# Squared distance of rows: a second load ahead of the entry barrier, and the result stored by two queues

## The chip, the cores and the metric

The kernel runs on one core of a Trainium2 chip. The metric is the device time of one execution in microseconds, of which the median of several runs is given. A profile is taken of one execution; its span goes from the first instruction to the last one on the core, and the device time also holds what lies around that span.

## The reference

```python
batch, dim = 1024, 4096
x, y = float32 [1024, 4096], float32 [1024, 4096]

def reference(x, y, axis):          # axis = -1
    return np.sum((x - y) ** 2, axis=axis).astype(np.float32)
```

Two arrays of 16.78 MB each are read, and 1024 numbers, 4 KB, are written.

## The kernel before

**Layout.** Partition p holds the 8 rows 8p to 8p+7 of x and y side by side, 32,768 columns in all (lines 60 and 61). The result is a tile `results` of 128 partitions by 8 columns, one column for each row of a partition, and goes back to the output with 32 bytes per partition (line 62).

**Loads.** SP issues all of them, in one queue, through the helper `load` (line 106 to 109), each with a semaphore of its own that counts to 16. The columns of x are cut in eight loads (`xw`, line 72), those of y in ten (`yw` and two narrow ones that are kept for the end, lines 73 and 74). The loop at lines 111 to 117 makes the order: x0 (4096 columns), x1 (12288), y0 (16256), x2, y1, and so on to two last y loads of 192 and 128 columns. X and Y hold six rows each (H, line 65), so loads beyond the sixth row wait on SP until the squares of the first two rows are done (line 220).

**The entry barrier.** Every engine begins with a drain and a barrier that all engines pass together. `Program.early` (line 29) takes the instructions that were recorded so far and puts them into the entry block, ahead of the named engine's first drain. Line 120 records one load, x0, and line 121 moves it ahead of SP's drain. SP issues the remaining loads after the barrier (lines 122 and 123).

**Arithmetic.** DVE waits for the loads of a piece and subtracts in place (`sub`, line 175); ACT waits for that difference, squares it and adds it up along the columns (`square`, line 181), one number for each piece; where a row has several pieces DVE adds these numbers (`complete`, line 188). The very last piece is squared and summed on DVE itself (line 204). All writers of `results` that end last count on the semaphore `sums`.

**The end.** SP waits until `sums` has its full count, issues the store of the whole tile (lines 231 and 232), clears the program's semaphores in one range (`close`, line 44) and waits for the store's 16 increments on `stored` (line 45). The semaphores that are cleared are those made by `prog.semaphore`, a range from the first to the last; `stored` is not among them and is counted back to 0 by the last wait.

Of the kernel before, what the change touches and what calls it, by code (L numbers as in the profile page):

```python
# [47 lines left out]
def kernel(tc, x, y, axis, out):  # L48
    nc = tc.nc
    P = nc.NUM_PARTITIONS  # L50
# [11 lines left out]
    ov = out.rearrange("(p r) -> p r", p=P)  # L62
# [5 lines left out]
    results = nc.alloc_sbuf_tensor("results", [P, R], F32).ap()  # L68
# [22 lines left out]
    prog = Program(nc, tc)  # L91
    stored = nc.alloc_semaphore("stored")
    diffs = prog.semaphore("diffs")
    acts = prog.semaphore("acts")
    sums = prog.semaphore("sums")
    n = dict(diffs=0, acts=0, sums=0)

    def home(c0, c1):
        h0 = c0 % H
        return slice(h0, h0 + c1 - c0)  # L100
# [5 lines left out]
    def load(landed, src, dst, name, c0, c1):  # L106
        sem = prog.semaphore("%s%d" % (name, len(landed)))
        nc.sync.dma_start(out=dst[:, home(c0, c1)], in_=src[:, c0:c1]).then_inc(sem, 16)  # L108
        landed.append(((c0, c1), sem))
# [7 lines left out]
        order.append((landed_y, yv, Y, "y", c0, c1))  # L117

    todo = list(order)
    load(*todo.pop(0))  # L120
    prog.early(mybir.EngineType.SP)
    while todo and todo[0][5] <= H:
        load(*todo.pop(0))
# [62 lines left out]
    def complete(r):  # L186
        nc.vector.wait_ge(acts, squared[row_parts[r][-1]])
        nc.vector.tensor_reduce(  # L188
            out=results[:, r : r + 1],
            in_=parts_of(r, len(row_parts[r])),  # L190
            axis=mybir.AxisListType.X,
            op=add,
        ).then_inc(sums, 1)
        n["sums"] += 1

    for j, (c0, c1) in enumerate(ys):
        final = j == len(ys) - 1
        wait_loaded(c1, landed_y[j][1])
        for piece in pieces_of(j, c0, c1):
            sub(*piece)  # L200
            r = piece[0] // D
            if final:
                nc.vector.wait_ge(diffs, n["diffs"])
                nc.vector.tensor_tensor_reduce(  # L204
                    out=Y[:, home(*piece)],
# [22 lines left out]
                complete(r)  # L228
    complete(7)

    nc.sync.wait_ge(sums, n["sums"])
    nc.sync.dma_start(out=ov, in_=results).then_inc(stored, 16)
    prog.close(nc.sync, stored, 16)


# [33 lines left out]
```

## Time and profile before

| | us |
|---|---|
| median of three runs | 84.13 (83.96 to 84.15) |
| the profiled execution, device time | 83.96 |
| the profiled execution, span | 82.63 |
| DVE busy | 36.8 |
| ACT busy | 33.4 |
| first DMA packet starts | 0.998 |
| the last load has landed | 80.25 |
| the last reduction ends | 81.15 |
| SP issues the store | 81.18 |
| the store's 16 increments land | 82.43 to 82.60 |

A row of the span's 40 slices gives the busy share of each slice in tenths; a slice is 2.07 us long. DMA packets count in the slice in which they start. SP's DMA-issuing instructions do not count as busy time; their rows stand in the timeline as SPq. In the text, x0, x1, y0 and so on are the loads in the order in which the kernel makes them for each array.

### The profile page before, as it was taken

The numbers are of one execution on the slowest core, as the hardware profiler recorded it, in microseconds if no ns is written. First come the engines' busy times: TensorE is split into PE (matmuls) and PEld (weight loads), VectorE is DVE, ScalarE is ACT, GpSimd is POOL, SyncE is SP. The second block draws the span as 40 slices with busy tenths as digits, with TensorE's granted clock in tenths as the row PEclk, the third lists the DMA queues.
The fourth block names the chain that finished last, engine by engine and source line by source line (L and its number), as shares of the span: only waits on it lengthen the run. The fifth ranks groups of instructions, "written<-read, shape, count | busy, mean of one in ns | idle before, by whom it ended". The sixth has DMA issues, their size and how long they took to land.

```text
span 82.6 us, 136 instructions
## 1 busy us (share of the span) xinstructions
DVE 36.8 (45%) x27; ACT 33.4 (40%) x41; POOL 0.2 (0%) x4
## 2 busy tenths in 40 slices
DVE  0000000000000000000299999999189996989992
ACT  3300000000000000000000979889896999899991
POOL 0000000000000000000000000000000000000000
DMA  5998998888999991999599699969979799999960
GB/s 127 389 500 381 595 547 381 381 381 381 504 504 504 504 504 63 441 504 504 254 508 508 286 476 508 476 286 508 423 339 509 339 437 440 426 402 416 395 220 2
DMA packets 2736, 33.56 MB, mean 406 GB/s; under 512 B 432, under 2 KB 1328, under 8 KB 1712
## 3 DMA queue, kind: packets, MB, share of 16 engines
q1 hardware_dynamic: 2736, 33.56, 95.9%
HBM read 33.55 MB, written 0.00 MB: 406 GB/s over the span
## 4 chain that ended last, share of the span: by engine, by line
DMA 63%; SPq 16%; DVE 12%; ACT 4%; issue 1%
DMA Y<-in_y_dram 63%; SPq L108 16%; DVE X L175 11%; ACT X L181 4%; DVE Y L204 0%; DVE results L188 0%; SPq L220 0%; DVE results L204 0%
## 5 line engine op out<-in xcount | busy, mean ns | idle before, releaser
L175 DVE TENSOR_TENSOR X<-X,Y 128x2048 f32<-128x2048 f32 (+10 forms) x21 | 36.2, 1780 | 44.3 <-DMA Y<-in_y_dram 44.3
L181 ACT ACTIVATE X<-X 128x2048 f32<-128x2048 f32 (+9 forms) x20 | 31.2, 1559 | 46.1 <-DVE X L175 46.0
L181 ACT ACTIVATION_READ_ACCUMULATOR X<-X 128x1 f32 x20 | 3.7, 186 | 0.0
L181 ACT ACT_TABLE_LOAD x1 | 1.3, 1283 | 1.4 <-PEq L19 1.4
L188 DVE TENSOR_REDUCE results<-parts 128x1 f32<-128x2 f32 (+2 forms) x4 | 0.4, 152 | 0.0
L204 DVE CUSTOM_DVE_ANT_0 Y<-X,parts 128x128 f32<-128x128 f32 x1 | 0.4, 352 | 0.0
L250 POOL MEMSET const-bfloat16-1.0<- 128x1 bf16 x1 | 0.1, 101 | 0.0
L250 POOL MEMSET const-uint8-127<- 128x1 uint8 x1 | 0.1, 101 | 0.0
L250 POOL MEMSET const-float32-0.0<- 128x1 f32 x1 | 0.1, 98 | 0.2 <-issue 0.2
L250 POOL MEMSET const-float32-1.0<- 128x1 f32 x1 | 0.1, 98 | 0.0
L204 DVE DVE_READ_ACCUMULATOR2_ANT results<- 128x1 f32 x1 | 0.1, 83 | 0.0
## 6 DMA issues: line engine op xcount, KB each, us to landing
Y<-in_y_dram SPq DMA_DIRECT2D x1, 8128.0 KB, 39.0
X<-in_x_dram SPq DMA_DIRECT2D x1, 6144.0 KB, 20.2
X<-in_x_dram SPq DMA_DIRECT2D x1, 4096.0 KB, 48.3
Y<-in_y_dram SPq DMA_DIRECT2D x1, 4096.0 KB, 57.5
X<-in_x_dram SPq DMA_DIRECT2D x1, 2736.0 KB, 13.3
X<-in_x_dram SPq DMA_DIRECT2D x1, 2048.0 KB, 7.1
Y<-in_y_dram SPq DMA_DIRECT2D x1, 1392.0 KB, 19.0
Y<-in_y_dram SPq DMA_DIRECT2D x1, 1312.0 KB, 16.1
```

The source lines that it names most:

```text
L108: nc.sync.dma_start(out=dst[:, home(c0, c1)], in_=src[:, c0:c1]).then_inc(sem, 16)
L175: nc.vector.tensor_sub(out=a, in0=a, in1=Y[:, home(c0, c1)]).then_inc(diffs, 1)
L181: nc.scalar.activation(out=a, in_=a, func=Square, accum_out=acc).then_inc(acts, 1)
L188: nc.vector.tensor_reduce(out=results[:, r : r + 1], in_=parts_of(r, len(row_parts[r])), axis=mybir.AxisListType.X, op=add,).then_inc(sums, 1)
L204: nc.vector.tensor_tensor_reduce(out=Y[:, home(*piece)], in0=X[:, home(*piece)], in1=X[:, home(*piece)], scale=1.0, scalar=parts_of(r, 1), ...
L250: nc = _bacc.Bacc("TRN2", target_bir_lowering=False, num_devices=1)
```

## The change

Two edits. The loop that records loads ahead of `early` now takes two loads, x0 and x1, so that SP issues both ahead of its drain for the entry barrier and starts with y0 behind it. At the end, the store is cut by partitions: ACT waits for the sums, issues the store of partitions 64 to 127 on its own queue and then counts a new semaphore `begun`; SP waits for the sums, issues the store of partitions 0 to 63, waits for `begun`, and then clears the semaphores and waits for 32 increments of `stored`. `begun` keeps SP from clearing `sums` before ACT has passed its wait for it.

```diff
@@ -93,6 +93,7 @@
     sums = prog.semaphore("sums")
+    begun = prog.semaphore("begun")
     n = dict(diffs=0, acts=0, sums=0)
@@ -117,7 +118,8 @@
     todo = list(order)
-    load(*todo.pop(0))
+    for _ in range(2):
+        load(*todo.pop(0))
     prog.early(mybir.EngineType.SP)
     while todo and todo[0][5] <= H:
         load(*todo.pop(0))
@@ -228,9 +230,15 @@
     complete(7)
 
+    half = P // 2
+    nc.scalar.wait_ge(sums, n["sums"])
+    nc.scalar.dma_start(out=ov[half:P], in_=results[half:P]).then_inc(stored, 16)
+    nc.scalar.sem_inc(begun, 1)
     nc.sync.wait_ge(sums, n["sums"])
-    nc.sync.dma_start(out=ov, in_=results).then_inc(stored, 16)
-    prog.close(nc.sync, stored, 16)
+    nc.sync.dma_start(out=ov[0:half], in_=results[0:half]).then_inc(stored, 16)
+    nc.sync.wait_ge(begun, 1)
+    prog.close(nc.sync, stored, 32)
```

## The prediction

> **What bounds the kernel now.** I read the 40 slices first, then the chain of waits, then the two ends of the span closely, because the change touches only those ends.
>
> ```profile
> DMA  5998998888999991999599699969979799999960
> GB/s 127 389 500 381 595 547 381 381 381 381 504 504 504 504 504 63 441 504 504 254 508 508 286 476 508 476 286 508 423 339 509 339 437 440 426 402 416 395 220 2
> DMA 63%; SPq 16%; DVE 12%; ACT 4%; issue 1%
> ```
>
> The DMA engines carry the program: 33.55 MB, with hardly an empty slice. The zeros and low digits inside the row are packets counted at their start (a packet of the second load lasts 1.8 us), not pauses. Only the first slice and the last two are really thin. So I cut the span by hand into windows (columns: length, busy time of DVE, ACT and POOL, granted clock, DMA share, GB/s):
>
> ```profile
> 0.00:0.99 0.99, 0.00 (x0) 0.00 (x0) 0.20 (x4) 1.00 0.00 0
> 7.00:21.00 14.00, 0.00 (x0) 0.00 (x0) 0.00 (x0) 1.00 0.91 393
> 21.00:79.75 58.75, 35.48 (x22) 30.94 (x35) 0.00 (x0) 1.00 1.01 428
> 80.05:82.01 1.96, 1.04 (x5) 0.91 (x6) 0.00 (x0) 1.00 0.00 0
> 82.01:82.23 0.22, 0.00 (x0) 0.00 (x0) 0.00 (x0) 1.00 0.35 19
> 82.23:82.63 0.40, 0.00 (x0) 0.00 (x0) 0.00 (x0) 1.00 0.00 0
> ```
>
> The reader is to see three parts. First 0.99 us in which nothing moves (the first packet starts at 0.998). Then 79 us in which the loads flow. Then a tail from 80.05 on: 1.1 us of arithmetic on the last pieces and 1.4 us of storing. The tail in the chain of waits (start, length, what) and the store's row among the DMA issues (from the start of its issue to its landing, 1.4 us):
>
> ```profile
> 66.94 13.12 DMA Y<-in_y_dram
> 80.05 0.02 issue
> 80.08 0.57 DVE X L175 x2
> 80.65 0.03 issue
> 80.67 0.35 DVE Y L204
> 81.03 0.01 DVE results L204
> 81.03 0.12 DVE results L188
> out_dram<-results SPq DMA_DIRECT2D x1, 4.0 KB, 1.4
> ```
>
> **The head: the second load ahead of the barrier.** SP's rows in the timeline of the first microseconds:
>
> ```profile
> 0.00 0.38 SPq L108 DMA_DIRECT2D X<-in_x_dram  x1
> 1.43 0.33 SPq L108 DMA_DIRECT2D X<-in_x_dram  x1
> 1.81 0.44 SPq L108 DMA_DIRECT2D Y<-in_y_dram  x1
> ```
>
> SP issues x0, its drain for the barrier starts at 0.425 and is the last to arrive, and the barrier (three rounds, line 19 and line 250) lets it go on to x1 at 1.433: 1.008 us from drain to next issue. After the change x1 is issued at 0.425, so the drain starts one issue and one gap later, 0.328 + 0.048 = 0.376, at 0.801. 1.008 later, at 1.81, comes y0, where it stands now (1.812). By the dearer issue row (0.436 for y0) it would be 1.92. So x1 is issued 1.008 us earlier, y0, x2 and y1 0 to 0.11 later, and the other engines leave the barrier 0.38 to 0.49 later.
>
> What is x1 worth 1.008 us earlier? Nothing, I say: x0 occupies all 16 engines until x1's packets follow at 6.5 without a gap (its landings are complete at 7.12), and x1 at 1.433 is 5 us ahead of its turn already. The cover is those 5 us of x0; with x0 over before 2.43 (1.433 plus the 0.998 that x0 needs to its first packet), the gain would be up to 1.008. The barrier's 0.38 to 0.49 falls on POOL's constants, on DVE, first needed at 40.86, and on ACT's table load, 1.438 plus 1.283, which moves to about 1.8 to 3.1 while ACT's first square is at 45.32: 42 us of cover. y0 is issued at 1.8 to 1.9 for a turn after 21. Against a gain stands one possible loss: x1's issue now runs before x0's first packet exists (0.998), where it ran at 1.433 beside the flow. The rows nearest are y0's, x2's and y1's issues from 1.8 to 3.2: the packets that start beside them take 0.61 to 0.65 us, as later ones do (0.61). So I take 0, and keep +0.38 (x0's first packet pushed back by a whole issue and gap) for the range. I find no gain here below 0.
>
> **The tail: two stores.** The path of the store now, from the trace's single rows: the last reduction ends at 81.149; SP's issue starts at 81.177 (0.348 long); the first packet starts at 82.019 (0.842 after the issue's start); 144 packets, 9 on each of 16 engines, have started by 82.213 (0.194); the last increment of the store's semaphore lands at 82.60 (0.387 after the last packet); SP's last wait is through at 82.613.
>
> SP's half. The issue and the way to the first packet are taken as they are. An issue here does not grow with the bytes: 0.328 for x1 (49,152 bytes a partition), 0.377 for x0 (16,384), 0.348 for the store (32). But each makes one packet for each of 128 partitions, so this trace can't exclude that it grows with partitions; then up to half the issue, 0.174, is saved. Each engine has 4 rows and not 8. One engine's 8 rows take about 0.047 (first packet of all 82.019, first completion packet 82.066), half of that is 0.024. SP's half thus lands 0.02 earlier, at best 0.20.
>
> ACT's half. ACT is idle from 80.957 and waits for the same count at 81.149, so it starts at 81.18 as SP does. No row shows a DMA issued by ACT. The bounds are SP's two ways to a first packet on idle DMA engines: 0.842 (the store, 18 issues into the program) and 0.998 (x0, the first issue of its queue, a load). ACT's store is the first on its queue, so I take 0.998: +0.156. Then 82.175 + 0.194 - 0.024 = 82.345 for its last packet and 0.387 more to land: 82.732, against 82.60. That is **+0.13**; with 0.842 it is -0.02.
>
> The completions: one semaphore takes 32 increments and not 16. The 16 now arrive between 82.43 and 82.60, about one every 11 ns. Bounds: 0, if increments of two stores interleave as the last two loads' did (between 80.01 and 80.05 their landings overlap at no slower rate), or a second 0.17 behind the first. With ACT 0.156 later the two rows of increments lie end to end anyway, so I take 0 and keep +0.17.
>
> Do the two halves get in each other's way on the engines? The window 82.01 to 82.23 above shows the store's packets filling 0.35 of 0.22 us on 16 engines, so two thirds of that time is free and the halves can lie beside each other: 0.
>
> A rule stands against this edit. The Trainium skill, "DMA: Bandwidth & Descriptors", section "Rules for kernel authors", says not to bother with two transfers to disjoint partition halves, since both spray over the same engines and serialize; taken strictly, ACT's 0.17 of packets would follow all of SP's and the sum would be an estimated 0.17 worse than by the window's row.
>
> The waits added. SP's wait for ACT's issue (begun): behind it on SP stand only the clearing of semaphores (now 81.577, 0.068 long) and the final wait, and nobody waits for those. ACT's increment should come at 81.18 + 0.377 + 0.05 = 81.61, so the clearing ends near 81.7, hidden under the landing at 82.6 to 82.7; the cover is 0.9 us. ACT's wait for the sums has only the store and that increment behind it.
>
> Sum on the profiled execution: 0 (head) + 0.13 (ACT's half) + 0 (increments, begun) = span 82.63 + 0.13 = 82.76; with the 1.33 us that lie around the span (83.96 - 82.63) 84.09. That execution was the fastest of three, 0.17 under the median, so against the median it is 84.13 + 0.13, about **84.27**.
>
> **The rivals.** About 0.3% (0.25 us) is what a measurement of this kernel can tell from no change.
>
> First, ACT's half is as quick as SP's warm store and halving pays: from -0.02 (packets alone) to -0.20 (issue by partitions too), so 83.93 to 84.11. For it: both engines are idle and released at the same time, the 16 DMA engines are empty. Against: the issue rows show no growth with bytes, and ACT's queue is unused before. Even at its best it stays inside 0.25 us; only with a head effect that I can't see would it be faster.
>
> Second, slower: the second store's completions come behind the first's. Its place is the stretch from 82.2 to 82.6, its price 0.17 for 16 increments more on top of ACT's 0.156 later start, 0.33 less 0.02, so 84.44. It decides as soon as ACT's first packet and the queueing together exceed 0.25, hence ACT's 0.156 with 0.12 of queueing is enough. For it: the final wait needs all 32, the later of two queues counts, and nothing else lies beside it. Against: the overlap at 80.01 to 80.05.
>
> Third, x1's early issue holds back x0's first packet by up to 0.38: every load moves by it, since the flow has no slack, and the time is 84.13 + 0.38 = 84.51, with ACT's 0.13 as much as 84.64. Against: the issue rows beside running packets.
>
> Fourth, the early issue really feeds the engines sooner: bounded by 1.008 (83.12), with 5 us of x0 in front of it very unlikely.
>
> **How the numbers follow.** Forecast (a loss of about 0.13, not tellable from none; own range 84.15 to 84.38) 0.45; ACT quick 0.22; second store's completions behind 0.18; x0 held back 0.11; the gain at the head 0.04. Faster by over 0.3%: the last case and half of ACT's quick case at its best end with scatter of the medians, 0.14. Slower: both slower cases, 0.29, and 0.09 of the forecast's upper edge, 0.38. The rest, 0.48, is within 0.3%. The range goes from 83.92 (ACT quick at its best) to 84.62 (x0 held back and ACT late).
>
> **What would show it.** Right: x0's first packet near 1.0 and x1's issue at 0.43, y0's issue at 1.8 to 1.9, no gap between x0's and x1's packets, the last load landing at 80.25 as now; in the tail an ACT issue starting at 81.18 with its first packet 0.9 to 1.0 later and the last of 32 increments at 82.7. An ACT packet as early as SP's speaks for the first rival; increments of one store waiting for the other's for the second; x0's first packet at 1.3 for the third. Wrong altogether would be the prediction if ACT's first issue costs something that no row of SP's shows (the one thing ACT fetches in this trace, its table, takes 1.28), or if the 1.33 us outside the span change because a second queue is in use.

## The result and the profile after

The changed kernel takes 84.70 us in the median (84.57 to 84.73), the kernel before 84.04 in the runs beside it: a ratio of 1.0076, 95% interval 1.0056 to 1.0096, or some 0.65 us slower. The forecast of 84.27 and the upper end of its range, 84.62, were both too low.

The profiled execution took 84.73 us with a span of 83.39, against 83.96 and 82.63: 0.76 us longer; what lies outside the span is as before (1.34 and 1.33). The first windows of the changed kernel's span (columns: stretch, length, DVE, ACT, POOL busy, granted clock, DMA share, GB/s) look as they did before:

```profile
0.00:1.00 1.00, 0.00 (x0) 0.00 (x0) 0.20 (x4) 1.00 0.00 0
7.00:21.00 14.00, 0.00 (x0) 0.00 (x0) 0.00 (x0) 1.00 0.92 398
21.00:79.75 58.75, 35.28 (x21) 30.69 (x35) 0.00 (x0) 1.00 1.00 426
```

Nothing moves in the first microsecond (first packet 1.008, before 0.998), and the flow has the same rate. SP's rows in the timeline show that x1's issue moved (it is the second of the two):

```profile
0.00 0.86 SPq L109 DMA_DIRECT2D X<-in_x_dram  x2
1.92 0.33 SPq L109 DMA_DIRECT2D Y<-in_y_dram  x1
```

The end of the chain of waits of the changed kernel (start, length, what):

```profile
67.19 13.10 DMA Y<-in_y_dram
80.29 0.02 issue
80.31 0.57 DVE X L177 x2
80.89 0.03 issue
80.91 0.35 DVE Y L206
81.26 0.01 DVE results L206
81.27 0.09 DVE results L190
```

The arithmetic behind the last loads is the same, but starts 0.23 us later. It waits for the last load but one, which landed at 80.292 and not at 80.052; the last one landed at 80.505 and not at 80.251. The last reduction ends at 81.362 instead of 81.149, which is 0.21 of the 0.76 us. The other 0.55 lie behind it. The two store issues in the timeline, their rows among the DMA issues (last column: us from the start of the issue to the landing), and the windows around their packets:

```profile
81.39 0.53 SPq L239 DMA_DIRECT2D out_dram<-results  x1
81.39 0.54 ACTq L236 DMA_DIRECT2D out_dram<-results  x1
```

```profile
out_dram<-results SPq DMA_DIRECT2D x1, 2.0 KB, 1.7
out_dram<-results ACTq DMA_DIRECT2D x1, 2.0 KB, 2.0
```

```profile
81.39:82.55 1.16, 0.00 (x0) 0.00 (x0) 0.00 (x0) 1.00 0.00 0
82.55:82.74 0.19, 0.00 (x0) 0.00 (x0) 0.00 (x0) 1.00 0.20 11
82.74:82.82 0.08, 0.00 (x0) 0.00 (x0) 0.00 (x0) 1.00 0.00 0
82.82:83.01 0.19, 0.00 (x0) 0.00 (x0) 0.00 (x0) 1.00 0.20 11
83.01:83.39 0.38, 0.00 (x0) 0.00 (x0) 0.00 (x0) 1.00 0.00 0
```

The reader is to see two things that no row of before had. Both engines are released together, at 81.39, but an issue of half as many partitions takes 0.53 and 0.54 us and not 0.35, and SP's first packet starts 1.17 us after the issue's start and not 0.84. And the packets come in two groups with an empty stretch between them: ACT's first packet starts 1.434 us after its issue's start, 0.27 behind SP's.

So three questions were open. Was the later last load the work of the early x1? Why is SP's own half slower? Why is ACT's half later still?

### The profile page after: what moved, and what is told of

It is laid out like the page before. It is cut to its first block, busy times and chain, and to the rows that moved or that the text cites. A ratio compares the mean times of both kernels' runs of the same rounds, so it can differ in the third digit from the quotient of the medians.

```text
span 83.4 us, 138 instructions
## 1 busy us (share of the span) xinstructions
DVE 36.7 (44%) x27; ACT 33.4 (40%) x41; POOL 0.2 (0%) x4
## 4 chain that ended last, share of the span: by engine, by line
DMA 63%; SPq 16%; DVE 12%; ACT 4%; issue 1%
DMA Y<-in_y_dram 63%; SPq L109 16%; DVE X L177 11%; ACT X L183 4%; DVE Y L206 0%; DVE results L190 0%; SPq L222 0%; DVE results L206 0%
```

## The experiments

Edits are against the kernel before unless another is named, `...` marks lines left out (the line that makes the semaphore `begun` is left out throughout), and ratios are against the kernel before in runs on the same chip. "Tail" is the time from the first store issue's start to the last increment of the store's semaphore: 1.42 us before (81.177 to 82.597), 1.97 in the changed kernel (81.390 to 83.358).

**The early load alone.**

```diff
-    load(*todo.pop(0))
+    for _ in range(2):
+        load(*todo.pop(0))
```

> The second load ahead of the barrier, the store as before. Theory 'held back': x1's issue at 0.425 us, straight behind x0's, pushes back x0's packets on the one DMA engine served last (in the changed kernel its first packet started at 1.864 us, the latest one before at 1.491), that engine stays behind to the end, and the last load lands 0.2 to 0.3 us later than before (80.45 to 80.55, not 80.25), time +0.2 to +0.3 us. Rival 'accident': the late engine was this one execution's, the last load lands at 80.25 within 0.1, time within 0.1 us of before. Rival 'gain': x1 earlier feeds the engines sooner, last load before 80.2, time below before.

The ratio is 1.0000 (0.9986 to 1.0014), medians 84.15 and 84.16. The profiled execution happened to be the slowest of the kernel's twelve (84.47), and its last load landed later than that of any other profile:

```profile
67.53 13.06 DMA Y<-in_y_dram
80.59 0.02 issue
80.61 0.57 DVE X L176 x2
```

The last load lands at 80.755 here, later than either theory said, and between 80.25 and 80.58 in the profiles of all kernels with one early load (80.47 with the split alone). The sixteenth packet of the program, the last before the engines begin their second ones at 2.1, starts at 1.862 here and 1.864 in the changed kernel, but at 1.887 in the kernel with one early load and the split store: it is not x1 that delays it. The scatter is there from the first load on: x0 has landed at 7.12 to 7.15 us in five of the profiles with one early load and at 7.28 to 7.41 in the other six; with two early loads it was 7.33 and 7.35. So "held back" falls, since its 0.2 to 0.3 us lie outside the interval of the ratio (0.12 us either way), and "accident" holds in its time: the landing of the last load scatters by some tenths from one execution to the next, the kernel before had been profiled at the early end of that (80.25), and the early load costs and brings nothing that these runs can tell.

**The split alone.** The change's second edit without its first (the edit is against the changed kernel):

```diff
-    for _ in range(2):
-        load(*todo.pop(0))
+    load(*todo.pop(0))
```

> Only x0 ahead of the barrier, the store split. If the two edits add, this has the rest of the 0.76 us by which the changed kernel's span is longer: last load at 80.25, end of the last reduction to end of span 2.0 us (before 1.48), time +0.5 to +0.6 us. If the split alone is cheap and only its meeting with the early load was dear, +0.13 us as predicted.

Ratio 1.0064 (1.0045 to 1.0083), median 84.72; by the ratio 0.54 us over before: all of the loss, within the interval. The tail is 1.96 us, with the same issues (0.525 and 0.542) and first packets (1.171 and 1.436) as in the changed kernel. The last load was 0.2 later than in the profile of before here too, which again belongs to the scatter.

**The whole store from ACT.**

```diff
-    nc.sync.wait_ge(sums, n["sums"])
-    nc.sync.dma_start(out=ov, in_=results).then_inc(stored, 16)
+    nc.scalar.wait_ge(sums, n["sums"])
+    nc.scalar.dma_start(out=ov, in_=results).then_inc(stored, 16)
+    nc.scalar.sem_inc(begun, 1)
+    nc.sync.wait_ge(begun, 1)
     prog.close(nc.sync, stored, 16)
```

> The whole store, 128 partitions, from ACT's queue alone; SP issues nothing there. Theory 'new queue': ACT's first DMA is slow by itself, issue about 0.54 us and first packet 1.2 to 1.4 us after the issue's start, time +0.4 to +0.6 us. Theory 'shared': only two issues at the same time slow each other, so this has an issue of 0.35 to 0.38 us, a first packet after 0.84 to 1.0 us, time 0 to +0.16 us.

Ratio 1.0003 (0.9989 to 1.0017). The windows of the store:

```profile
81.25:82.12 0.87, 0.00 (x0) 0.00 (x0) 0.00 (x0) 1.00 0.00 0
82.12:82.33 0.21, 0.00 (x0) 0.00 (x0) 0.00 (x0) 1.00 0.37 20
82.33:82.73 0.40, 0.00 (x0) 0.00 (x0) 0.00 (x0) 1.00 0.00 0
```

ACT's first DMA of the whole program takes 0.370 us to issue and 0.871 to its first packet, against 0.348 and 0.842 on SP; the tail is 1.44. ACT's queue, used for the first time, costs 0.02 to 0.03 us over SP's here, and "new queue" falls.

**One half from SP alone.** The lower half is stored as in the change, nothing by ACT; the upper half of the result is left out.

```diff
-    nc.sync.dma_start(out=ov, in_=results).then_inc(stored, 16)
+    nc.sync.dma_start(out=ov[0:64], in_=results[0:64]).then_inc(stored, 16)
```

> SP stores partitions 0 to 63 alone; the upper 512 numbers of the output are left out. Theory 'shape': a store of 64 partitions is dearer to issue, 0.53 us and a first packet after 1.17 us as SP's half had in the changed kernel. Theory 'shared': alone it has at most the 0.348 us issue and 0.842 us to the first packet of the whole store; if the issue grows with partitions, 0.17 to 0.25 us and 0.67 to 0.75 us.

```profile
81.31 0.53 SPq L232 DMA_DIRECT2D out_dram<-results  x1
```

```profile
81.31:82.47 1.16, 0.00 (x0) 0.00 (x0) 0.00 (x0) 1.00 0.00 0
82.48:82.66 0.18, 0.00 (x0) 0.00 (x0) 0.00 (x0) 1.00 0.21 12
82.66:83.04 0.38, 0.00 (x0) 0.00 (x0) 0.00 (x0) 1.00 0.00 0
```

With no second queue and half the bytes, SP's store has the same 0.526 us of issue and 1.167 to the first packet as in the changed kernel, and a tail of 1.69: 0.27 us longer than that of the whole store. "Shared" does not explain SP's half; the form with 64 partitions does.

**Which forms are dear.** Ten stores from SP after the sums, each waited for, and then thirteen more in a second kernel.

```diff
-    nc.sync.dma_start(out=ov, in_=results).then_inc(stored, 16)
-    prog.close(nc.sync, stored, 16)
+    count = 0
+    for rows in (128, 64, 64, 96, 96, 32, 32, 16, 16, 128):
+        nc.sync.dma_start(out=ov[0:rows], in_=results[0:rows]).then_inc(stored, 16)
+        count += 16
+        nc.sync.wait_ge(stored, count)
+    prog.close(nc.sync, stored, count)
```

> After the sums SP stores the tile's first n partitions ten times, each waited for before the next: n = 128, 64, 64, 96, 96, 32, 32, 16, 16, 128; the time as a whole says nothing. Theory 'shape': every store of 64 is dear (issue near 0.53 us, first packet near 1.17 us), the second as much as the first, and 128 stays at 0.35 and 0.84; what 96, 32 and 16 show tells whether it is a matter of not being 128. Theory 'first of its kind': a 64-partition issue is slow only once, because the issuing engine has not made that form before; the first 64 has 0.53, the second 0.35 us, and 96, 32 and 16 likewise dear only the first time if at all.

> More forms of store from SP after the sums, each waited for: partitions 0-128, 0-64, 64-128, 32-96, then 48 twice, 80 twice, 112 twice, 60 twice, and 0-64 at last. If 64 is dear for its number, 64-128, 32-96 and the last 0-64 take 0.46 to 0.53 us of issue and 1.1 to 1.2 us to the first packet, and 48, 80 and 112 (multiples of 16, as 96 is) 0.31 to 0.37 and 0.80 to 0.86. If it is a matter of where the partitions lie, only 0-64 and 64-128 are dear and 32-96 is not.

Lines of the timeline of the first kernel (128, then 64 twice, 96 and 32), and below them two of its windows, each from the start of an issue to just before its first packet:

```profile
81.40 0.35 SPq L234 DMA_DIRECT2D out_dram<-results  x1
82.83 0.53 SPq L234 DMA_DIRECT2D out_dram<-results  x1
84.55 0.47 SPq L234 DMA_DIRECT2D out_dram<-results  x1
86.21 0.36 SPq L234 DMA_DIRECT2D out_dram<-results  x1
89.01 0.31 SPq L234 DMA_DIRECT2D out_dram<-results  x1
```

```profile
81.40:82.24 0.84, 0.00 (x0) 0.00 (x0) 0.00 (x0) 1.00 0.00 0
82.83:84.00 1.17, 0.00 (x0) 0.00 (x0) 0.00 (x0) 1.00 0.00 0
```

All forms, from the trace's single rows of both kernels (first and second time of a form where it ran twice, us):

| partitions | issue | issue's start to first packet |
|---|---|---|
| 0-128 (three of them) | 0.348 to 0.350 | 0.840 to 0.846 |
| 0-112 | 0.317, 0.317 | 0.816, 0.813 |
| 0-96 | 0.363, 0.326 | 0.854, 0.821 |
| 0-80 | 0.317, 0.316 | 0.812, 0.811 |
| 0-64 (four of them) | 0.466 to 0.549 | 1.120 to 1.185 |
| 64-128 | 0.466 | 1.115 |
| 32-96 | 0.548 | 1.199 |
| 0-60 | 0.377, 0.327 | 0.798, 0.801 |
| 0-48 | 0.370, 0.325 | 0.861, 0.818 |
| 0-32 | 0.314, 0.314 | 0.806, 0.810 |
| 0-16 | 0.315, 0.314 | 0.806, 0.808 |

Among the counts tried it is the number 64, wherever the 64 partitions lie, the first time and the later ones. A form that is new costs 0.03 to 0.06 us more to issue once in some rows (64, 96, 48, 60); that is "first of its kind", and it is small. The counts tried below 64 and above it are all cheap. A transfer of 64 partitions here also moves 2 KB in all, but that is not it: in the split by columns below, each queue moves 2 KB and issues in 0.344 and 0.378. All these stores have 32 bytes per partition; other lengths with 64 partitions were not tried. Why 64 alone is dear no run here shows; it stays open.

**Both halves on SP.**

```diff
+    half = P // 2
...
-    nc.sync.dma_start(out=ov, in_=results).then_inc(stored, 16)
-    prog.close(nc.sync, stored, 16)
+    nc.sync.dma_start(out=ov[0:half], in_=results[0:half]).then_inc(stored, 16)
+    nc.sync.dma_start(out=ov[half:P], in_=results[half:P]).then_inc(stored, 16)
+    prog.close(nc.sync, stored, 32)
```

> Both halves of the store on SP's queue, one behind the other. 'Shape': two issues of 0.53 us, last packets about 0.55 us later than one half's (1.17 + 0.17 + 0.55 after the first issue's start), time +0.8 us. 'First of its kind': the second issue 0.35 us, time +0.6 us. If SP's queue were free of what the second queue costs, the second half would follow at 0.27 us and this equals the split over two queues.

Ratio 1.0111 (1.0094 to 1.0128), 0.95 us over before by the medians (85.07 and 84.12), above every number expected. The second issue starts at 81.912 when the first is done and takes 0.587 us; the tail is 2.33. "Shape" is the nearest; two dear issues in one queue are worse than one in each of two.

**The split by columns.**

```diff
+    nc.scalar.wait_ge(sums, n["sums"])
+    nc.scalar.dma_start(out=ov[:, 4:8], in_=results[:, 4:8]).then_inc(stored, 16)
+    nc.scalar.sem_inc(begun, 1)
...
-    nc.sync.dma_start(out=ov, in_=results).then_inc(stored, 16)
-    prog.close(nc.sync, stored, 16)
+    nc.sync.dma_start(out=ov[:, 0:4], in_=results[:, 0:4]).then_inc(stored, 16)
+    nc.sync.wait_ge(begun, 1)
+    prog.close(nc.sync, stored, 32)
```

> The store split over ACT and SP by columns (4 of 8 each), so that both halves keep 128 partitions, 16 bytes each. If the form with 64 partitions is the first half of the loss, both issues take 0.35 to 0.38 us here and the first packet of the first half comes 0.84 us after its issue's start. If two issues at once are the second half of the loss, the other half's packets come some 0.2 to 0.3 us behind it, time +0.25 to +0.35 us; if not, both come together and the time is within 0.1 us of before.

Ratio 1.0028 (1.0008 to 1.0047): 0.24 us, under half the loss of the split by partitions, but more than the 0.1 expected where both come together. The windows of its tail:

```profile
81.44:82.27 0.83, 0.00 (x0) 0.00 (x0) 0.00 (x0) 1.00 0.00 0
82.27:82.53 0.26, 0.00 (x0) 0.00 (x0) 0.00 (x0) 1.00 0.60 16
82.53:83.05 0.52, 0.00 (x0) 0.00 (x0) 0.00 (x0) 1.00 0.00 0
```

Two issues at once, of 128 partitions each, take 0.344 and 0.378 us, and their packets lie in one stretch of 0.24 us, ACT's 0.05 behind SP's. What remains is the last window: 0.49 us from the last packet to the last increment, 0.38 before. The 32 increments arrive as one row from 82.69 to 83.02, about 11 ns apart, where 16 took 0.17. The tail is 1.58 us, 0.16 longer. The row begins 1.25 us after SP's issue, as before, so the 0.16 fits what the second set of 16 increments takes; that these queue behind the first is inferred from the times and was not tested by itself.

**ACT's queue used beforehand.** The split store (its lines, as in the split alone, are left out here), with a load of 64 partitions by 8 columns issued by ACT behind the entry barrier.

```diff
+    nc.scalar.dma_start(out=scratch, in_=xv[0 : P // 2, 0:R]).then_inc(warmed, 16)
...
+    nc.scalar.wait_ge(warmed, 16)
```

> The split store over both queues, with ACT's queue used before: ACT loads 64 partitions by 8 columns of x into a scratch tile behind the entry barrier. 'New queue': ACT's half then comes as early as SP's, time 0.27 us under the plain split (+0.3 instead of +0.56 against before). 'First of its kind': ACT's issue drops from 0.54 to 0.35-0.38 us, SP's stays at 0.53. 'Shape' with two issues at once: nothing changes, +0.5 to +0.6 us.

Ratio 1.0077 (1.0061 to 1.0092), as the changed kernel. The early load of 64 partitions took 0.532 us to issue, so a load seems dear as well, though this one ran beside SP's issue of x1. Its 64 rows lie 131,072 bytes apart in memory, which speaks against the stores' 2 KB in one piece as the cause. ACT's store issue fell only from 0.542 to 0.498, began 0.065 us behind SP's because of its extra wait, and its first packet still came 0.27 us behind SP's. Nothing is gained, as "shape" said.

**One half from ACT alone.** Only ACT's store of the split is left; the lower half of the result is left out.

> ACT stores partitions 64 to 127 alone, SP nothing; the lower 512 numbers of the output are left out. In the changed kernel ACT's first packet came 1.434 us after its issue's start, 0.264 after SP's. If the two issues wait for each other on the way to the engines, alone it comes after 1.17 to 1.20 us, as SP's half alone (1.167). If ACT is slow with this form by itself, 1.43 us again.

```profile
81.18:82.36 1.18, 0.00 (x0) 0.00 (x0) 0.00 (x0) 1.00 0.00 0
82.36:82.54 0.18, 0.00 (x0) 0.00 (x0) 0.00 (x0) 1.00 0.22 12
82.54:82.93 0.39, 0.00 (x0) 0.00 (x0) 0.00 (x0) 1.00 0.00 0
```

Alone, ACT's first packet comes after 1.183 us, as SP's does; beside SP's half it came after 1.434. The 0.25 us are the meeting of two dear transfers; SP's half pays nothing for it (1.170 beside ACT's, 1.167 alone). Two cheap ones, by columns, are 0.05 apart. What holds ACT's back no run here shows.

**The cut moved to 96.** The change's own split with one number changed: SP stores 96 partitions, ACT 32 (the edit is against the split alone).

```diff
-    half = P // 2
+    half = 96
```

> The split over both queues with the cut moved: SP stores 96 partitions, ACT the upper 32. If the form with 64 partitions makes the loss, both issues are short here (0.31 to 0.37 us), the first packets come 0.81 to 0.90 us after the issues' start, and from SP's issue to the last landing pass 1.5 to 1.6 us (1.42 before, 1.97 with halves of 64), time +0.1 to +0.25 us. If any cut by partitions over two queues is dear, 1.9 us or more and +0.5 us.

```profile
81.46:82.31 0.85, 0.00 (x0) 0.00 (x0) 0.00 (x0) 1.00 0.00 0
82.31:82.53 0.22, 0.00 (x0) 0.00 (x0) 0.00 (x0) 1.00 0.38 19
82.53:83.10 0.57, 0.00 (x0) 0.00 (x0) 0.00 (x0) 1.00 0.00 0
```

Ratio 1.0016 (1.0002 to 1.0029), 0.13 us, with issues of 0.362 and 0.395 and a tail of 1.61. Most of the loss of 0.54 is gone by moving the cut. What is left fits the row of 32 increments, which also here come one behind the other (82.70 to 83.06). Here the packets of the two queues share one stretch as well, ACT's 0.04 behind SP's. No split that was tried is faster than the one store of 128 partitions.

## Why the prediction was wrong

Its verdict of "no change that can be told" and its range failed at the price of the two halves: a transfer of 64 partitions was taken to cost no more than one of 128, and the meeting of two of them to cost nothing. Its steps fared as follows.

**The head, 0: right.** x1 early alone gives a ratio of 1.0000 (0.9986 to 1.0014). x1's issue took 0.440 us and y0's came at 1.921, the dearer of the two values given (1.92). The third rival, x0 held back, looked true in the profile of the changed kernel, since the last load landed 0.25 later, although its own sign, x0's first packet at 1.3, was missing (1.008); the early load alone shows that it was scatter of single executions. The fourth, a gain, did not come either.

**"SP's half. The issue and the way to the first packet are taken as they are": wrong, and this is the failed step.** The prediction saw that every row had 128 partitions, and bounded the unknown form only downwards, by up to 0.174 saved, with nothing upwards. Measured alone, the half is 0.27 us longer to its landing (1.69 and 1.42), because a transfer of 64 partitions has 0.526 us of issue and 1.167 to its first packet, where 0.348 and 0.842 were taken over.

**ACT's half, +0.13 for a first use of its queue: wrong in its cause and too small.** First use costs 0.02 to 0.03 (the whole store from ACT). ACT's half was 0.27 behind SP's in landing, because ACT's transfer of the dear form comes later beside SP's: 1.183 to the first packet alone, 1.434 together. The terms that should have stood there are 0.27 for the form and 0.27 for the meeting: 0.54, which the split alone shows (1.0064, 0.54 us).

**The increments, 0 with +0.17 kept: right for the change, and the bound was the right size.** In the changed kernel SP's 16 are through at 83.09 and ACT's begin at 83.19, so neither waits. Where the packets lie together, by columns, the second 16 add 0.16. The overlap of the last two loads, which the prediction took as evidence against, concerned two semaphores and 16 increments each, and did not carry over to two stores on one semaphore.

**The wait on begun, hidden: right.** SP cleared the semaphores at 82.009, 0.064 long, with the last increment at 83.358.

**"Do the two halves get in each other's way on the engines": 0, right for the engines, and wrong as the whole price of the meeting.** By columns, and with 96 and 32 partitions, the packets of two queues lie side by side. But two halves of 64 get in each other's way before their packets, for 0.25 to 0.27 us, and the prediction had looked at the packets alone. The Trainium skill's advice in "DMA: Bandwidth & Descriptors", section "Rules for kernel authors", not to bother with halves, is borne out by every split here (0.13 to 0.95 us slower). Its reason, that halves serialize on the same 16 engines, fits the two groups of packets of the changed kernel in appearance only: the engines are empty for 0.08 us between them, so what held ACT's 64 partitions back lies ahead of the packets. The 0.17 that the prediction estimated from that rule is not the 0.54 that was measured.

The mechanism of the second rival, completions behind each other, was thus not what happened, though the price it named (84.44) was nearer than the forecast. The nearest price on record, 84.64 with x0 held back and ACT late, was near by luck: the early load alone shows no such loss at the head.

Some slips of the prediction change none of this: its range ends at 84.62, where its own sum for that case is 84.64; 0.04 and half of 0.22 are 0.15 and not 0.14; and of the 32 packets that start from 1.8 to 3.2 us two took 0.68 and 0.88 us and not 0.61 to 0.65.

## What to carry to other kernels

When a transfer changes its form, the cost of its issue is unknown until a row with that form has been seen, and the unknown has to be bounded upwards too: half the bytes were 0.27 us slower here. The store of 4 KB at the end of this kernel is nearly all fixed time (0.84 us to the first packet, 0.2 of packets, 0.38 to land); cutting it saved nothing in any form tried, and a second part seems to add its own row of increments. Before a later landing in one profile is put down to an edit, run that edit alone: the last load's landing moved by up to 0.5 us between profiled executions, while the medians of the kernel before and of that with the early load alone agreed.

## What the runs showed of the hardware

- A DMA of 64 partitions by 8 columns (32 bytes each) took 0.466 to 0.549 us to issue and 1.115 to 1.199 to its first packet on SP with nothing else under way, and about the same on ACT (0.523 and 1.183 alone), at three places of the tile. With 16, 32, 48, 60, 80, 96, 112 and 128 partitions it was 0.314 to 0.377 and 0.798 to 0.861. A load of 64 partitions took 0.532 to issue, beside another issue. The cause is open.
- Two such transfers issued at once from SP and ACT are 0.27 us apart in their first packets; two of 128 partitions only 0.05, 96 and 32 partitions 0.04.
- Increments of one semaphore by 16 DMA engines arrive about 11 ns apart, and where the packets of two DMAs lie together, their 32 increments on one semaphore form one row of 0.33 to 0.37 us.
- ACT's queue, used for the first time at the end of the program, was 0.03 us slower to its first packet than SP's.
